# Row sums of absolute values: a partition takes eight neighbouring rows, the transpose goes, and the last row is loaded and reduced in pieces

## Chip, cores, metric

One core of one Trainium2 chip. The metric is the device time of one execution in microseconds (us), the median over repeated executions. Every run reported here is with a granted TensorE clock of 1.00.

In the profile lines DVE is VectorE, ACT is ScalarE, PE is TensorE, and SPq is the queue of SyncE, which issues the DMAs (the transfers between HBM, the chip's main memory, and the on-chip memory of 128 partitions). A packet is the piece of a DMA that one of the core's 16 DMA engines moves at a time. A load has landed when all its packets have; an instruction that waits for it can then start.

## What is computed

```python
batch, dim = 1024, 4096
x = np.random.randn(batch, dim).astype(np.float32)      # fixed seed
out = np.sum(np.abs(x), axis=-1).astype(np.float32)     # shape (1024,)
```

The input has 16.78 MB, the output 4 KB.

## The kernel before

Row 128t+p of the input goes to partition p as its tile t. The last tile (t = 7) is loaded in two parts: its first 3072 columns before everything else, its last 1024 columns after everything else. VectorE sums columns 0 to 3071 of each tile, ScalarE the other 1024. The sums then lie across partitions in an order that the output hasn't; TensorE transposes them into 8 rows of 128. The code here is shortened; "..." marks what is left out.

```python
x_t = x.rearrange("(t p) m -> t p m", p=P)
out_v = out.rearrange("(t p) -> t p", p=P)
v_cols = (dim * 3) // 4
...
nc.sync.dma_start(out=x_tiles[last][:, :v_cols], in_=x_t[last, :, :v_cols])
for t in range(ntiles - 1):
    nc.sync.dma_start(out=x_tiles[t], in_=x_t[t])
nc.sync.dma_start(out=x_tiles[last][:, v_cols:], in_=x_t[last, :, v_cols:])

for t in range(ntiles):
    nc.vector.tensor_reduce(out=sums_v[:, t:t+1], in_=x_tiles[t][:, :v_cols], ...)   # abs, add
for t in range(ntiles):
    nc.scalar.activation(out=chunk, in_=chunk, func=Abs, accum_out=sums_s[:, t:t+1])
nc.vector.tensor_add(out=sums_all, in0=sums_v, in1=sums_s)
nc.tensor.transpose(sums_T_psum, final_sums, identity)
nc.vector.tensor_copy(out=out_sbuf, in_=sums_T_psum)
nc.sync.dma_start(out=out_v, in_=out_sbuf)
```

Of the kernel before, what the change touches and what calls it, by code (L numbers as in the profile page):

```python
# [1 line left out]

# [5 lines left out]


@with_exitstack
def kernel(
    ctx: ExitStack,
    tc: tile.TileContext,
    x: bass.AP,
    axis: int,
    out: bass.AP,
):
    nc = tc.nc
    P = nc.NUM_PARTITIONS  # L20

    batch, dim = x.shape
    assert axis in (-1, 1), f"only the last-axis reduction is supported, got {axis}"
    assert batch % P == 0, f"batch ({batch}) must be a multiple of {P}"

    ntiles = batch // P

    x_t = x.rearrange("(t p) m -> t p m", p=P)
    out_v = out.rearrange("(t p) -> t p", p=P)

    v_cols = (dim * 3) // 4
    if ntiles == 1 or dim < 256:
        v_cols = dim
    s_cols = dim - v_cols

    data_pool = ctx.enter_context(tc.tile_pool(name="data", bufs=1))
    acc_pool = ctx.enter_context(tc.tile_pool(name="acc", bufs=1))
    psum_pool = ctx.enter_context(tc.tile_pool(name="psum", bufs=1, space=bass.MemoryType.PSUM))

    identity = acc_pool.tile([P, P], mybir.dt.float32)  # L40
    make_identity(nc, identity)

    sums_v = acc_pool.tile([P, ntiles], mybir.dt.float32)
    if s_cols > 0:
        sums_s = acc_pool.tile([P, ntiles], mybir.dt.float32)
    sums_all = acc_pool.tile([P, ntiles], mybir.dt.float32)

    x_tiles = [
        data_pool.tile([P, dim], x.dtype, name=f"x_tile_{t}", bufs=1)
        for t in range(ntiles)  # L50
    ]

    last = ntiles - 1
    if s_cols > 0:
        nc.sync.dma_start(out=x_tiles[last][:, :v_cols], in_=x_t[last, :, :v_cols])  # L55
    else:
        nc.sync.dma_start(out=x_tiles[last], in_=x_t[last])

    for t in range(ntiles - 1):
        nc.sync.dma_start(out=x_tiles[t], in_=x_t[t])  # L60

    if s_cols > 0:
        nc.sync.dma_start(
            out=x_tiles[last][:, v_cols:], in_=x_t[last, :, v_cols:]
        )

    for t in range(ntiles):
        nc.vector.tensor_reduce(  # L68
            out=sums_v[:, t : t + 1],
            in_=x_tiles[t][:, :v_cols],  # L70
            axis=mybir.AxisListType.X,
            op=mybir.AluOpType.add,
            apply_absolute_value=True,
        )
    if s_cols > 0:
        for t in range(ntiles):
            chunk = x_tiles[t][:, v_cols:]
            nc.scalar.activation(  # L78
                out=chunk,
                in_=chunk,  # L80
                func=mybir.ActivationFunctionType.Abs,
                accum_out=sums_s[:, t : t + 1],
            )

    if s_cols > 0:
        nc.vector.tensor_add(out=sums_all, in0=sums_v, in1=sums_s)  # L86
        final_sums = sums_all
    else:
        final_sums = sums_v

    sums_T_psum = psum_pool.tile([ntiles, P], mybir.dt.float32)
    nc.tensor.transpose(sums_T_psum, final_sums, identity)  # L92

    out_sbuf = acc_pool.tile([ntiles, P], mybir.dt.float32)
    nc.vector.tensor_copy(out=out_sbuf, in_=sums_T_psum)  # L95

    nc.sync.dma_start(out=out_v, in_=out_sbuf)


# [1 line left out]
_INS = ['x', 'axis']  # L101
_OUTS = [((1024,), 'float32')]
#: Inputs that are plain numbers.
_NUMBERS = {'axis': -1}


# [26 lines left out]
```

## Time and profile before

| What | us | Where it is read |
|---|---|---|
| median time | 50.14 (50.00 to 50.22, 15 runs) | runs |
| span of the profiled run | 48.33 | page |
| first load lands | 7.45 | timeline: VectorE's first reduction starts |
| last load lands | 42.91 | timeline: ScalarE's last ACTIVATE starts |
| store issued | 46.16 | timeline |
| store landed | 47.42 | semaphore records |

### The profile page before, as it was taken

The numbers are of one execution on the slowest core, as the hardware profiler recorded it, in microseconds if no ns is written. First come the engines' busy times: TensorE is split into PE (matmuls) and PEld (weight loads), VectorE is DVE, ScalarE is ACT, GpSimd is POOL, SyncE is SP. The second block draws the span as 40 slices with busy tenths as digits, with TensorE's granted clock in tenths as the row PEclk, the third lists the DMA queues.
The fourth block names the chain that finished last, engine by engine and source line by source line (L and its number), as shares of the span: only waits on it lengthen the run. The fifth ranks groups of instructions, "written<-read, shape, count | busy, mean of one in ns | idle before, by whom it ended". The sixth has DMA issues, their size and how long they took to land.

```text
span 48.3 us, 93 instructions
## 1 busy us (share of the span) xinstructions
PE 0.4 (1%) x1; PEld 0.1 (0%) x1; DVE 27.3 (56%) x10; ACT 10.5 (22%) x17; POOL 0.7 (1%) x6
## 2 busy tenths in 40 slices
PE   0000000000000000000000000000000000000300
PEld 0000000000000000000000000000000000000000
DVE  0000008990899079907990699169915992599410
ACT  3600000000810071007200620063005300594000
POOL 5000000000000000000000000000000000000000
DMA  0779999999999999999999999999999998800000
GB/s 0 132 264 356 407 414 434 434 434 420 434 434 434 434 434 434 407 434 434 434 434 420 434 434 434 420 434 420 434 434 434 434 420 342 346 3 0 0 3 0
DMA packets 1312, 16.78 MB, mean 347 GB/s; under 512 B 152, under 2 KB 160, under 8 KB 288
## 3 DMA queue, kind: packets, MB, share of 16 engines
q1 hardware_dynamic: 1312, 16.78, 83.4%
HBM read 16.78 MB, written 0.00 MB: 347 GB/s over the span
## 4 chain that ended last, share of the span: by engine, by line
DMA 77%; DVE 8%; SPq 7%; issue 1%; PE 1%; DVEq 0%
DMA x_tile<-in_x_dram 77%; DVE sums_v L68 7%; SPq L60 6%; SPq L55 1%; PE sums_T_psum L92 1%; DVE out_sbuf L95 1%; DVE sums_all L86 0%; DVEq L86 0%
## 5 line engine op out<-in xcount | busy, mean ns | idle before, releaser
L68 DVE TENSOR_REDUCE sums_v<-x_tile 128x1 f32<-128x3072 f32 x8 | 26.8, 3353 | 18.2 <-DMA x_tile<-in_x_dram 18.2
L78 ACT ACTIVATE x_tile<-x_tile 128x1024 f32<-128x1024 f32 x8 | 8.5, 1057 | 32.8 <-DMA x_tile<-in_x_dram 32.7
L78 ACT ACTIVATION_READ_ACCUMULATOR x_tile<-x_tile 128x1 f32 x8 | 1.5, 186 | 0.0
L78 ACT ACT_TABLE_LOAD x1 | 1.3, 1283 | 0.7 <-PEq L114 0.7
L92 PE MATMUL sums_T_psum<-identity,sums_all 128*8 128x128 f32 x1 | 0.4, 372 | 45.4 <-DVE sums_all L86 45.4
L95 DVE COPY out_sbuf<-sums_T_psum 8x128 f32<-8x128 f32 x1 | 0.3, 279 | 0.6 <-PE sums_T_psum L92 0.6
masks.py:199 POOL TENSOR_SCALAR_AFFINE_SELECT identity<-identity 128x128 f32<-128x128 f32 x1 | 0.3, 294 | 0.1
L86 DVE TENSOR_TENSOR sums_all<-sums_v,sums_s 128x8 f32<-128x8 f32 x1 | 0.2, 167 | 0.1
masks.py:197 POOL MEMSET identity<- 128x128 f32 x1 | 0.2, 205 | 0.3 <-POOLq L114 0.3
L92 PEld LDWEIGHTS sums_T_psum<-identity,sums_all 128*8 128x8 f32 x1 | 0.1, 83 | 45.4 <-issue 45.4
L114 POOL MEMSET const-float32-0.0<- 128x1 f32 x1 | 0.1, 99 | 0.2 <-issue 0.2
L114 POOL MEMSET const-bfloat16-1.0<- 128x1 bf16 x1 | 0.1, 102 | 0.0
L114 POOL MEMSET const-uint8-127<- 128x1 uint8 x1 | 0.1, 102 | 0.0
L114 POOL MEMSET const-float32-1.0<- 128x1 f32 x1 | 0.1, 99 | 0.0
## 6 DMA issues: line engine op xcount, KB each, us to landing
x_tile<-in_x_dram SPq DMA_DIRECT2D x7, 2048.0 KB, 26.5
x_tile<-in_x_dram SPq DMA_DIRECT2D x1, 1536.0 KB, 6.7
x_tile<-in_x_dram SPq DMA_DIRECT2D x1, 512.0 KB, 35.4
out_dram<-out_sbuf SPq DMA_DIRECT2D x1, 4.0 KB
```

Source lines behind the costliest of these rows:

```text
L55: nc.sync.dma_start(out=x_tiles[last][:, :v_cols], in_=x_t[last, :, :v_cols])
L60: nc.sync.dma_start(out=x_tiles[t], in_=x_t[t])
L68: nc.vector.tensor_reduce(out=sums_v[:, t : t + 1], in_=x_tiles[t][:, :v_cols], axis=mybir.AxisListType.X, op=mybir.AluOpType.add, apply_a ...
L78: nc.scalar.activation(out=chunk, in_=chunk, func=mybir.ActivationFunctionType.Abs, accum_out=sums_s[:, t : t + 1],)
L86: nc.vector.tensor_add(out=sums_all, in0=sums_v, in1=sums_s)
L92: nc.tensor.transpose(sums_T_psum, final_sums, identity)
L95: nc.vector.tensor_copy(out=out_sbuf, in_=sums_T_psum)
L114: nc = _bacc.Bacc("TRN2", target_bir_lowering=False, num_devices=1)
```

## The change

Its intent: without a transpose the result can leave at once, and with the last row cut into small pieces little is left to do when the last byte lands. Partition p holds rows 8p to 8p+7, so its eight sums are neighbours in the output. Rows come in groups of 2, 2, 2 and 1; the eighth row comes in four pieces of falling size, and VectorE and ScalarE share each row about evenly. Core of the diff:

```diff
-    x_t = x.rearrange("(t p) m -> t p m", p=P)
-    out_v = out.rearrange("(t p) -> t p", p=P)
+    x_v = x.rearrange("(p t) m -> p t m", p=P)
+    out_v = out.rearrange("(p t) -> p t", p=P)
...
+    GROUPS = [(0, 2), (2, 4), (4, 6), (6, 7)]
+    CUTS = [(0, 1792), (1792, 2880), (2880, 3712), (3712, 4096)]
+    for a, b in GROUPS:
+        nc.sync.dma_start(out=xt[:, a:b, :], in_=x_v[:, a:b, :])
+    for a, b in CUTS:
+        nc.sync.dma_start(out=xt[:, last, a:b], in_=x_v[:, last, a:b])
...
+    h = (dim * 15) // 32
+    for t in range(last):
+        vec(t, 0, h, sv[:, t : t + 1])
+        act(t, h, dim, ss[:, t : t + 1])
+    vec(last, 0, 896, sv[:, last:])
+    act(last, 896, 1792, ss[:, last:])
+    vec(last, 1792, 2432, v2)
+    act(last, 2432, 2880, s2)
+    act(last, 2880, 3712, s3)
+    nc.vector.tensor_add(out=total[:, :last], in0=sv[:, :last], in1=ss[:, :last])
+    # pre = sv + ss + v2 and pre2 = pre + s2, for the last row
...
+    vec(last, 3712, 4096, v3)
+    # total[:, last] = v3 + s3 + pre2
...
-    nc.tensor.transpose(sums_T_psum, final_sums, identity)
-    nc.vector.tensor_copy(out=out_sbuf, in_=sums_T_psum)
-    nc.sync.dma_start(out=out_v, in_=out_sbuf)
+    nc.sync.dma_start(out=out_v, in_=total)
```

`vec` is the same `tensor_reduce` with absolute values and `act` the same `Abs` ACTIVATE with an accumulator as before.

More of the change, by code (lines that the diff above doesn't have):

```diff
@@ L22 @@
     batch, dim = x.shape
-    assert axis in (-1, 1), f"only the last-axis reduction is supported, got {axis}"
-    assert batch % P == 0, f"batch ({batch}) must be a multiple of {P}"
-    ntiles = batch // P
-    x_t = x.rearrange("(t p) m -> t p m", p=P)
-    out_v = out.rearrange("(t p) -> t p", p=P)
-    v_cols = (dim * 3) // 4
-    if ntiles == 1 or dim < 256:
-        v_cols = dim
-    s_cols = dim - v_cols
-    data_pool = ctx.enter_context(tc.tile_pool(name="data", bufs=1))
-    acc_pool = ctx.enter_context(tc.tile_pool(name="acc", bufs=1))
@@ L38 @@
-    psum_pool = ctx.enter_context(tc.tile_pool(name="psum", bufs=1, space=bass.MemoryType.PSUM))
-    identity = acc_pool.tile([P, P], mybir.dt.float32)
-    make_identity(nc, identity)
-    sums_v = acc_pool.tile([P, ntiles], mybir.dt.float32)
-    if s_cols > 0:
-        sums_s = acc_pool.tile([P, ntiles], mybir.dt.float32)
-    sums_all = acc_pool.tile([P, ntiles], mybir.dt.float32)
-    x_tiles = [
-        data_pool.tile([P, dim], x.dtype, name=f"x_tile_{t}", bufs=1)
-        for t in range(ntiles)
-    ]
@@ L53 @@
-    last = ntiles - 1
-    if s_cols > 0:
-        nc.sync.dma_start(out=x_tiles[last][:, :v_cols], in_=x_t[last, :, :v_cols])
-    else:
-        nc.sync.dma_start(out=x_tiles[last], in_=x_t[last])
-    for t in range(ntiles - 1):
-        nc.sync.dma_start(out=x_tiles[t], in_=x_t[t])
-    if s_cols > 0:
-        nc.sync.dma_start(
-            out=x_tiles[last][:, v_cols:], in_=x_t[last, :, v_cols:]
-        )
-    for t in range(ntiles):
+    nt = batch // P
+    f32 = mybir.dt.float32
+    add = mybir.AluOpType.add
@@ new lines @@
+    x_v = x.rearrange("(p t) m -> p t m", p=P)
+    out_v = out.rearrange("(p t) -> p t", p=P)
+    data = ctx.enter_context(tc.tile_pool(name="data", bufs=1))
+    acc = ctx.enter_context(tc.tile_pool(name="acc", bufs=1))
+    last = nt - 1
+    xt = data.tile([P, nt, dim], f32, name="xt")
+    sv = acc.tile([P, nt], f32, name="sv")
+    ss = acc.tile([P, nt], f32, name="ss")
+    v2 = acc.tile([P, 1], f32, name="v2")
+    v3 = acc.tile([P, 1], f32, name="v3")
+    s2 = acc.tile([P, 1], f32, name="s2")
@@ new lines, with vec @@
+    s3 = acc.tile([P, 1], f32, name="s3")
+    pre = acc.tile([P, 1], f32, name="pre")
+    pre2 = acc.tile([P, 1], f32, name="pre2")
+    total = acc.tile([P, nt], f32, name="total")
+    GROUPS = [(0, 2), (2, 4), (4, 6), (6, 7)]
[4 more added lines that the diff above has]
+        nc.sync.dma_start(out=xt[:, last, a:b], in_=x_v[:, last, a:b])
+    def vec(t, a, b, out_):
@@ L68 @@
         nc.vector.tensor_reduce(
-            out=sums_v[:, t : t + 1],
-            in_=x_tiles[t][:, :v_cols],
+            out=out_,
+            in_=xt[:, t, a:b],
             axis=mybir.AxisListType.X,
-            op=mybir.AluOpType.add,
+            op=add,
             apply_absolute_value=True,
         )
-    if s_cols > 0:
-        for t in range(ntiles):
-            chunk = x_tiles[t][:, v_cols:]
-            nc.scalar.activation(
-                out=chunk,
-                in_=chunk,
-                func=mybir.ActivationFunctionType.Abs,
-                accum_out=sums_s[:, t : t + 1],
-            )
@@ L85, with act @@
-    if s_cols > 0:
-        nc.vector.tensor_add(out=sums_all, in0=sums_v, in1=sums_s)
-        final_sums = sums_all
-    else:
-        final_sums = sums_v
-    sums_T_psum = psum_pool.tile([ntiles, P], mybir.dt.float32)
-    nc.tensor.transpose(sums_T_psum, final_sums, identity)
-    out_sbuf = acc_pool.tile([ntiles, P], mybir.dt.float32)
-    nc.vector.tensor_copy(out=out_sbuf, in_=sums_T_psum)
-    nc.sync.dma_start(out=out_v, in_=out_sbuf)
+    def act(t, a, b, out_):
+        nc.scalar.activation(
+            out=xt[:, t, a:b],
+            in_=xt[:, t, a:b],
+            func=mybir.ActivationFunctionType.Abs,
+            accum_out=out_,
+        )
@@ new lines @@
+    h = (dim * 15) // 32
[8 more added lines that the diff above has]
+    nc.vector.tensor_add(out=total[:, :last], in0=sv[:, :last], in1=ss[:, :last])
+    nc.vector.scalar_tensor_tensor(
+        out=pre, in0=sv[:, last:], scalar=ss[:, last:], in1=v2, op0=add, op1=add
+    )
@@ L101 @@
+    nc.vector.tensor_add(out=pre2, in0=pre, in1=s2)
+    vec(last, 3712, 4096, v3)
+    nc.vector.scalar_tensor_tensor(
+        out=total[:, last:], in0=v3, scalar=s3, in1=pre2, op0=add, op1=add
+    )
+    nc.sync.dma_start(out=out_v, in_=total)
 _INS = ['x', 'axis']
```

## The prediction

> **What bounds the kernel now.** I first read the whole page for its shape, then the chain of work that ended last in order of time, then the timeline of the last 12 us, and at the end the trace's list of DMA packets (each with its size and duration). The page says that this is a stream of 16.78 MB with little work beside it:
>
> ```profile
> DVE  0000008990899079907990699169915992599410
> ACT  3600000000810071007200620063005300594000
> DMA  0779999999999999999999999999999998800000
> GB/s 0 132 264 356 407 414 434 434 434 420 434 434 434 434 434 434 407 434 434 434 434 420 434 434 434 420 434 420 434 434 434 434 420 342 346 3 0 0 3 0
> ```
>
> Each column is 1.2 us. The DMA engines are full from the third slice to the thirty-fifth, at 434 GB/s in the middle; after that there are five slices in which they do nearly nothing. There is a ramp in front, a tail behind, and neither compute engine is busy throughout. The chain in order of time says what the tail consists of (start, duration, what):
>
> ```profile
> 4.19 0.04 issue
> 4.23 37.41 DMA x_tile<-in_x_dram
> 41.64 0.02 issue
> 41.66 3.36 DVE sums_v L68
> ...
> 45.13 0.18 DVE sums_all L86
> 45.31 0.14 issue
> 45.44 0.39 PE sums_T_psum L92
> 45.83 0.02 issue
> 45.85 0.28 DVE out_sbuf L95
> ```
>
> The chain follows the seventh full tile, which lands at 41.66. The reader is to see that everything after 41.66 is serial: a reduction of 3072 columns over all 128 partitions, one addition, a transpose on TensorE, a copy out of PSUM. The timeline adds what the chain does not show, when the very last bytes land and when the result goes out:
>
> ```profile
> 41.66 1.06 ACT L78 ACTIVATE x_tile<-x_tile 128x1024 f32<-128x1024 f32 x1 [3.74 <-DMA x_tile<-in_x_dram]
> 41.66 3.35 DVE L68 TENSOR_REDUCE sums_v<-x_tile 128x1 f32<-128x3072 f32 x1 [1.54 <-DMA x_tile<-in_x_dram]
> 42.63 0.19 ACT L78 ACTIVATION_READ_ACCUMULATOR x_tile<-x_tile 128x1 f32 x1
> 42.91 1.06 ACT L78 ACTIVATE x_tile<-x_tile 128x1024 f32<-128x1024 f32 x1
> ...
> 46.16 0.37 SPq L97 DMA_DIRECT2D out_dram<-out_sbuf  x1
> ```
>
> The 512 KB remainder of the last tile was issued at 7.45 and lands 35.4 us later by the DMA issues, at about 42.9; ScalarE starts on it at 42.91. So the input ends at E = 42.9, the store is issued at 46.16, and E to store is **3.25 us**. From the store's issue to the span's end at 48.3 are 2.15 us, and the measured 50.16 us are 1.85 us above the span; both are in either kernel.
>
> **What the Trainium skill says, and whether the trace agrees.** (1) "VectorE: DVE Perf Modes", the perf-mode tier table: tensor_reduce runs at one element per cycle in every format. The trace agrees: 3353 ns for 3072 columns is 3072/0.96 = 3200 ns plus 153 ns. (2) "ScalarE: Activation LUTs", What ACT_TABLE_LOAD costs: an ACTIVATE with immediates takes 186 ns + 0.833 N. For N = 1024 that is 1039; the trace has 1057, so I use 204 + 0.833 N, plus 0.09 us for the accumulator read of 186 ns, which overlaps by half (42.63 to 42.82 behind an ACTIVATE that ends at 42.72). (3) "DMA: Bandwidth & Descriptors", Latency and other measured facts: copies of 128 rows of 16 KiB keep 207 GB/s each way at a row pitch of 512 KiB but fall to 164 at 2 MiB and 103 at 4 MiB. The change moves the pitch from 16 KB to 128 KB, below all those, so this speaks for no loss; the trace of before, with its 16 KB pitch, cannot confirm it. (4) Same page, Specifications: under 512 B a DMA engine does read-modify-write. The new store has runs of 32 bytes; before had 512, so no line of this trace shows what those cost.
>
> **The change, part by part.** *Layout of the input.* Partition p now holds rows 8p to 8p+7, the bytes are the same, and the stream is the same length if the engines keep their rate. The packets give the rate: 611 ns for 16 KB, 460 ns for the undisturbed ones of 12 KB, 159 ns for 4 KB. That is 0.0368 ns per byte plus about 8 ns a packet, one engine at a time, no gap between DMAs (tiles land every 4.89 us = 8 x 611 ns). Each engine takes 8 of the 128 partitions. The last row of a partition is now cut in four pieces of 7168, 4352, 3328 and 1536 bytes: 272 + 168 + 131 + 65 = 636 ns instead of 611, and eight times that is +0.2 us. Before paid one such cut (460 + 159 - 611 = 8 ns, times 8, is 0.06), so net **+0.15**. Larger packets in front (32 KB if the two rows of a group are one run) give back under 0.1. The start may differ: in before the first DMA's packets of 12 KB took up to 1.56 us and then 460 to 670, so the engines finished them about 1.1 us later than 8 x 460 would have them. About half is latency of the first packet and returns. The rest could come from the odd 12 KB row or from 16 engines starting together; I give it a mean gain of **0.1**.
>
> *The tail.* With E' the landing of the last piece (1536 B x 8 per engine), the earlier landings follow from the packet times: third piece E'-0.52 (8 x 65), second E'-1.57 (8 x 131 earlier), first E'-2.91 (8 x 168 earlier), row 6 E'-5.09 (8 x 272 earlier). VectorE at 153 ns + N/0.96: row 6, 1920 columns, 2.15 us, ends at E'-2.94; 896 columns, 1.09 us, from E'-2.91 to E'-1.82; 640 columns, 0.82 us, from E'-1.57 to E'-0.75. Then three small ops. In before the add of 8 columns took 0.17 and came 0.10 after the reduction, so 0.27 each and 0.8 together: to E'+0.05, hardly later than the last piece. Its 384 columns take 0.55: to E'+0.6. ScalarE: row 6, 2176 columns, 2.02 + 0.09 us, ends at E'-2.98; 896 columns 1.04 us, ends at E'-1.87; 448 columns 0.67 us, ends at E'-0.9; 832 columns 0.99 us from E'-0.52, ends at E'+0.47, ahead of VectorE's 0.6. The last sum of three waits for both: 0.10 + 0.17, so E'+0.87; the store is issued 0.03 later as in before (the copy ends 46.13, issue 46.16): **E'+0.9 to 0.95**. Against E+3.25 this removes **2.3 us**. Of it, cutting the reduction that straddled the end is worth 42.9 to 45.0 less 0.6, about 1.5; add, transpose and PSUM copy (45.03 to 46.13, 1.1 us) against one last sum (0.27) the other 0.8.
>
> *Beside the stream.* Per row VectorE needs 2.15 us and ScalarE 2.11, against 4.89 for the stream, so rows in pairs (4.3 us per 9.8) leave both idle over half the time; the new split of columns is worth nothing until the end. The identity on GpSimd disappears, before 1.3 us and off the path: nothing.
>
> *The store.* 128 runs of 32 bytes over 16 engines in place of 8 runs of 512 over 8. In before those packets took 28 to 53 ns; eight in a row on an engine are about 0.3 us more, with nothing else in flight: **+0.25**.
>
> Sum: 50.16 - 2.3 + 0.15 - 0.1 + 0.25 = 48.16, and I say **48.1 us**.
>
> **The rivals.** *A. The new pitch slows the stream.* The groups stride 128 KB between partitions and the 16 engines work half a megabyte apart. For it: in before the engines spread evenly in time (their first-DMA ends lie 0.57 us apart, one 16 KB packet is 0.61), which looks like streams avoiding one another, and power-of-two pitches are what the skill warns of. Against it: 128 KB is under the pitches where the skill saw a loss, and each run is 32 KB long. Five per cent on 41 us would cost 2 us and eat the gain: 50.2. *B. The wait moves rather than vanishing.* VectorE's order in the tail is up to the scheduler; if a small op that waits for ScalarE's 832 columns stood ahead of the last reduction, the end would be E'+0.47+0.1+0.55+0.54 and 0.8 us would be given back: 48.9. In before the scheduler put the tile that lands first in front, so it orders by readiness, which speaks against this. *C. The end of the stream suffers from small packets and the store from small writes.* Packets of 1536 B and 32 B may have a floor above my line; twice my estimates is +0.4: 48.5. *D. The slow start goes with the 12 KB rows.* Then up to 0.6 us more is won: 47.6.
>
> **Range and chances.** The tail's 2.3 us is built from measured durations and I trust it to 0.3. The start (0.6 either way at most) and the store (0.3) are the next terms; together they make about 0.6 around 48.1. A is the one large risk, at one in ten for more than 1 us, and gives the longer upper arm. So 47.2 to 49.0. Two per cent under 50.16 is 49.16: faster 0.89, same 0.09, slower 0.02.
>
> **What would show it right or wrong.** Right: a middle of the stream at 434 GB/s; input ending within 0.5 us of 42.9; the last VectorE reduction of 384 columns starting within 0.1 us of the last landing; the store issued about 0.9 us after it; about 2.3 us from there to the end. Wrong: GB/s under 420 in the middle slices (A); VectorE's last reduction held by a small op that waits for ScalarE (B); more than 2.6 us from the store's issue to the end, or the four pieces spread over more than 5.5 us (C); an input that ends before 42.3 (D).

## The result

The changed kernel takes **47.13 us** (47.02 to 47.57, 10 runs) against 50.14: a ratio of 0.9412, 95% interval 0.9391 to 0.9434. Ratios are the mean time of one kernel's fast runs over that of the other's fast runs of the same rounds, so not quite the ratio of the medians quoted. The direction was right, and 3.0 us were won where 2.0 were forecast; the time lies just below the range of 47.2 to 49.0.

The first profile of the changed kernel fell on one of its longer runs (47.42). Its busy share of the DMA engines and its GB/s, in 40 slices of 1.14 us:

```profile
DMA  0909999999999979899899999995999899995000
GB/s 0 431 29 460 460 460 460 460 460 460 460 460 431 460 316 402 373 431 431 373 460 460 460 460 460 460 460 230 460 388 431 349 408 397 413 394 207 0 4 0
```

Against before, the ramp at the front looks shorter: the fourth slice is at full rate, where before it took until the seventh. At the end three slices are empty instead of five. Single slices shouldn't be read finely here: packets of 32 KB are booked whole (431, then 29), and the 460 lies above the packets' own rate of 16 x 32768 B / 1213 ns = 432 GB/s. How much of the ramp is really gone is therefore read from the first landing, below. The chain that ended last (start, duration, what):

```profile
4.14 38.38 DMA xt<-in_x_dram
42.51 0.02 issue
42.54 0.56 DVE v L53
...
43.19 0.22 DVE total L84
```

The DMA now runs to 42.5 and 0.9 us of work follow it, where 41.6 and 4.5 us stood before. A second profile of the same kernel, of a run of 47.14 us and so nearer to the median, gives the tail in the timeline:

```profile
37.17 2.15 DVE L53 TENSOR_REDUCE sv<-xt 128x1 f32<-128x1920 f32 x1 [0.68 <-DMA xt<-in_x_dram]
39.51 1.08 DVE L53 TENSOR_REDUCE sv<-xt 128x1 f32<-128x896 f32 x1
40.73 0.82 DVE L53 TENSOR_REDUCE v<-xt 128x1 f32<-128x640 f32 x1
41.65 0.22 DVE L79 SCALAR_TENSOR_TENSOR pre<-sv,ss,v 128x1 f32<-128x1 f32 x1
...
41.79 0.90 ACT L62 ACTIVATE xt<-xt 128x832 f32<-128x832 f32 x1 [0.39 <-DMA xt<-in_x_dram]
42.26 0.55 DVE L53 TENSOR_REDUCE v<-xt 128x1 f32<-128x384 f32 x1
42.59 0.19 ACT L62 ACTIVATION_READ_ACCUMULATOR xt<-xt 128x1 f32 x1
42.92 0.22 DVE L84 SCALAR_TENSOR_TENSOR total<-v,s,pre 128x1 f32<-128x1 f32 x1
43.17 0.35 SPq L87 DMA_DIRECT2D out_dram<-total  x1
```

Row 6 lands at 37.17, and each piece is worked off by about the time the next one lands. The last piece lands at 42.26 and VectorE starts on it at once. ScalarE's piece of 832 columns is read out by 42.78, before VectorE is done at 42.81. The sum of three follows at 42.92 and the store at 43.17, 0.91 us after the last landing. The tail is as predicted (0.90 to 0.95). What differs from the forecast therefore lies ahead of 42.26, in the stream, or behind 43.17, in the store.

### The profile page after: what moved, and what is told of

It is laid out like the page before. It is cut to its first block, busy times and chain, and to the rows that moved or that the text cites. A ratio compares the mean times of both kernels' runs of the same rounds, so it can differ in the third digit from the quotient of the medians.

```text
span 45.6 us, 94 instructions
## 1 busy us (share of the span) xinstructions
DVE 17.9 (39%) x14; ACT 18.4 (40%) x21; POOL 0.2 (0%) x4
## 4 chain that ended last, share of the span: by engine, by line
DMA 84%; SPq 7%; DVE 2%; issue 1%; DVEq 0%
DMA xt<-in_x_dram 84%; SPq L48 4%; SPq L50 3%; DVE v L53 1%; DVE total L84 0%; DVEq L84 0%
## 5 line engine op out<-in xcount | busy, mean ns | idle before, releaser
L62 ACT ACTIVATE xt<-xt 128x2176 f32<-128x2176 f32 (+3 forms) x10 | 16.5, 1648 | 23.9 <-DMA xt<-in_x_dram 23.9
L53 DVE TENSOR_REDUCE sv<-xt 128x1 f32<-128x1920 f32 (+1 forms) x8 | 15.9, 2015 | 24.5 <-DMA xt<-in_x_dram 24.5
L62 ACT ACTIVATION_READ_ACCUMULATOR xt<-xt 128x1 f32 x10 | 1.9, 186 | 0.0
L53 DVE TENSOR_REDUCE v<-xt 128x1 f32<-128x640 f32 (+1 forms) x2 | 1.4, 686 | 0.6 <-DMA xt<-in_x_dram 0.4
```

What stands on the lines that cost most here:

```text
L53: nc.vector.tensor_reduce(out=out_, in_=xt[:, t, a:b], axis=mybir.AxisListType.X, op=add, apply_absolute_value=True,)
L62: nc.scalar.activation(out=xt[:, t, a:b], in_=xt[:, t, a:b], func=mybir.ActivationFunctionType.Abs, accum_out=out_,)
```

## The experiments

A measure for the start of the stream is needed. I take the **start overhead**: the landing of the first DMA less the time of its packets on one engine when they run undisturbed (8 packets, one for each of the engine's 8 partitions, of 460 ns for 12 KB, 611 for 16 KB, 1213 for 32 KB in the list of DMA packets that each trace keeps; 16 packets where two rows of a partition aren't adjacent in memory). Before it is 7.45 - 8 x 0.460 = 3.77 us, in the first profile of the changed kernel 12.80 - 8 x 1.213 = 3.10. That is already 0.67 us of the 1.0 that I missed. Three theories for it:

- **P**: pieces of 12 KB of a 16 KB row run badly wherever they stand, and the change has none of them at the start.
- **Q**: at the start of any stream the 16 engines disturb one another, and small packets take longer to get over it.
- **L**: only the addresses count; rows that are close together in HBM (16 KB from one partition to the next) start slowly, rows 128 KB apart do not.

All runs in one table, times in us. The landings, the store and the span are those of one profiled execution, the median time is that of all. "First packets" are the size of the first DMA's packets, "pitch" the distance in HBM between the rows of neighbouring partitions.

| Run | first packets, pitch | first landing | overhead | last landing | store issued | span | median time |
|---|---|---|---|---|---|---|---|
| before | 12 KB, 16 KB | 7.45 | 3.77 | 42.91 | 46.16 | 48.33 | 50.14 |
| b_12k_second | 16 KB, 16 KB | 8.40 | 3.51 | 42.88 | 46.13 | 48.30 | 50.12 |
| b_loads_only | 12 KB, 128 KB | 6.84 | 3.16 | 42.35 | 45.59 | 47.77 | 49.51 |
| b_layout | 12 KB, 128 KB | 6.71 | 3.03 | 42.23 | 44.64 | 46.90 | 48.69 |
| b_dead_pe | 12 KB, 128 KB | 6.84 | 3.16 | 42.33 | 44.75 | 47.09 | 48.86 |
| changed kernel, first profile | 32 KB, 128 KB | 12.80 | 3.10 | 42.54 | 43.44 | 45.64 | 47.13 |
| a_oldlayout | 16 KB, 16 KB | 13.11 | 3.33 | 42.98 | 43.89 | 46.09 | 47.88 |
| a_pitch32k | 32 KB, 32 KB | 13.05 | 3.35 | 42.42 | 43.33 | 45.53 | 47.30 |
| a_flat32k | 32 KB, 128 KB | 12.89 | 3.19 | 42.29 | 43.19 | 45.40 | 47.15 |
| a_again | 32 KB, 128 KB | 12.85 | 3.15 | 42.26 | 43.17 | 45.36 | 47.12 |
| a_first16k | 16 KB, 128 KB | 7.97 | 3.08 | 42.20 | 44.45 | 46.66 | 48.50 |
| a_first12k | 12 KB, 128 KB | 6.69 | 3.01 | 42.12 | 43.02 | 45.22 | 47.19 |
| a_uncut2 | 32 KB, 128 KB | 12.69 | 2.99 | 41.88 | 44.34 | 46.54 | 48.41 |
| a_fused | 32 KB, 128 KB | 12.81 | 3.11 | 42.20 | 42.90 | 45.10 | 46.87 |

Three of these runs put sums in the wrong place on purpose (a_oldlayout, a_pitch32k, b_loads_only). They still compared as correct: sums of 4096 absolute normals have a mean of 0.798 x 4096 = 3268 and a spread of 0.603 x 64 = 39, so that two rows typically differ by one or two per cent and the comparison didn't see the exchange.

How far single profiles scatter can be read from the table: five profiles with 32 KB first at a pitch of 128 KB have overheads of 2.99 to 3.19, four with 12 KB at that pitch 3.01 to 3.16.

### b_12k_second: the 12 KB rows in second place

```diff
+    nc.sync.dma_start(out=x_tiles[0], in_=x_t[0])
...
     nc.sync.dma_start(out=x_tiles[last][:, :v_cols], in_=x_t[last, :, :v_cols])
...
-    for t in range(ntiles - 1):
+    for t in range(1, ntiles - 1):
```

> The kernel before with its first two loads exchanged: 16 KB rows of tile 0 first, the 12 KB part of the last tile second. Start overhead = landing of the first DMA minus 8 undisturbed packets of it; it was 7.45 - 8 x 0.460 = 3.77 us before and 12.80 - 8 x 1.213 = 3.10 after. Theory P (only 12 KB pieces of 16 KB rows run badly, wherever they stand): overhead of the first DMA 3.1, the second DMA takes 4.2 to 4.5 us instead of 3.7 between the two landings, time 50.1 as before. Theory Q (the start of any stream is disturbed until the 16 engines have spread out in time, and small packets take longer over it): overhead 3.4 to 3.7, the 12 KB packets then run at 460 ns, 3.7 us between the landings, time 49.8 to 50.1.

VectorE's first two reductions in the timeline of this run (start, duration, what; each starts as its load lands):

```profile
8.40 3.35 DVE L69 TENSOR_REDUCE sums_v<-x_tile 128x1 f32<-128x3072 f32 x1 [8.40 <-DMA x_tile<-in_x_dram]
12.22 3.35 DVE L69 TENSOR_REDUCE sums_v<-x_tile 128x1 f32<-128x3072 f32 x1 [0.46 <-DMA x_tile<-in_x_dram]
```

The 12 KB load takes 3.82 us between the landings, near the 3.7 of theory Q and far from the 4.2 of P: in second place such packets run well. The start with 16 KB packets has an overhead of 3.51, as Q has it. But the time is 50.12, unchanged: what the first landing gains on before, the second load loses. P falls; the old layout starts slowly with full rows too. Q stands so far, L too.

### a_first12k: the changed kernel with 12 KB packets first

```diff
-    GROUPS = [(0, 2), (2, 4), (4, 6), (6, 7)]
+    x_f = x_v.rearrange("p t m -> p (t m)")
+    xt_f = xt.rearrange("p t m -> p (t m)")
+    FLAT = [(0, 3072), (3072, 16384), (16384, 24576), (24576, 28672)]
...      # one dma_start for each range of FLAT
```

> The changed kernel with its first DMA cut to 12 KB of row 0 (the second takes the other 52 KB up to row 3, then rows 4 and 5, then 6): packets of 12 KB first, at the new pitch. Theories P and Q: overhead 3.6 to 3.8 as before, time 47.7 to 47.8. Theory L (pitch): overhead 3.1, time 47.1.

VectorE's first reduction in this run:

```profile
6.69 2.15 DVE L55 TENSOR_REDUCE sv<-xt 128x1 f32<-128x1920 f32 x1 [6.69 <-DMA xt<-in_x_dram]
```

And in the kernel before:

```profile
7.45 3.35 DVE L68 TENSOR_REDUCE sums_v<-x_tile 128x1 f32<-128x3072 f32 x1 [7.45 <-DMA x_tile<-in_x_dram]
```

Both wait for a first load of 12 KB per partition, issued at 0.73 and 0.74, and the one with rows 128 KB apart lands 0.76 us earlier. Overhead 3.01, time 47.19. Theories P and Q both said 3.6 to 3.8 and 47.7 or more; only L said this.

### a_first16k: one row in the first group

```diff
-    GROUPS = [(0, 2), (2, 4), (4, 6), (6, 7)]
+    GROUPS = [(0, 1), (1, 3), (3, 5), (5, 7)]
```

> The changed kernel with row groups of 1, 2, 2, 2 rows instead of 2, 2, 2, 1: the first DMA has packets of 16 KB at the new pitch of 128 KB. Theory P (12 KB pieces alone are bad) and theory L (the old pitch of 16 KB is bad): overhead 3.1, time 47.1 to 47.2. Theory Q (size of the first packets): overhead 3.4 to 3.7, time 47.5 to 47.8.

The overhead is 3.08, again with L against Q, and the stream ends at 42.20. But the time is 48.50, 1.3 us above what P and L said and 0.7 above the upper end of Q: a fault of my edit. VectorE in the timeline:

```profile
37.12 5.20 DVE L53 TENSOR_REDUCE sv<-xt 128x1 f32<-128x1920 f32 x3 [5.53 <-DMA xt<-in_x_dram]
42.24 0.81 DVE L53 TENSOR_REDUCE v<-xt 128x1 f32<-128x640 f32 x1
...
43.56 0.55 DVE L53 TENSOR_REDUCE v<-xt 128x1 f32<-128x384 f32 x1
44.21 0.22 DVE L84 SCALAR_TENSOR_TENSOR total<-v,s,pre 128x1 f32<-128x1 f32 x1
```

The last group now brings rows 5 and 6 together at 37.12. VectorE's three reductions from there (rows 5 and 6 and the first piece of row 7) run on to 42.3, past the last landing at 42.20; the later pieces queue behind them, and the last reduction starts at 43.56, 1.36 us after its data. The store comes 2.25 us after the last landing instead of 0.91. The run shows by accident that row 6 must come by itself: that small last group is worth 1.3 us.

### a_oldlayout: the changed kernel with the old row order

```diff
-    x_v = x.rearrange("(p t) m -> p t m", p=P)
+    x_v = x.rearrange("(t p) m -> p t m", p=P)
```

> The changed kernel reading its rows in the old order (row 128t+p to partition p), so the pitch is 16 KB and packets are 16 KB in all row groups; the sums come out in the wrong order on purpose. 24 more packets per engine at 8 to 9 ns are +0.2 us in any theory. Theory L (old pitch bad at the start): overhead 3.7, time 47.9 to 48.0. Theory P: overhead 3.1, time 47.3 to 47.4. Theory Q: overhead 3.4 to 3.7, time 47.6 to 48.0.

47.88 us, 0.75 more than the changed kernel. Of this 0.2 are the 24 additional packets per engine, and the overhead of 3.33 gives another 0.2. The rest is not in the start: in this profile packets of 4352 bytes late in the stream took up to 472 ns instead of 168, and the last landing was at 42.98. Whether such late disturbances belong to the old order stays open; all four executions took 47.69 to 47.93, more than the 47.5 that the two other terms give. The time fits L and Q alike; the overhead is lower than either had said for this pitch.

So the "only" in L isn't shown. At 128 KB the size of the first packets makes no clear difference (2.99 to 3.19), but at the old pitch the overhead is 3.77 with 12 KB, 3.51 with 16 KB and 3.33 here, where the first load is larger and also reads the two rows of a partition from places 2 MB apart. The runs don't separate these two. For this kernel the new pitch is thus worth only about 0.2 us at the start (3.33 against 3.15).

### a_pitch32k and a_flat32k: nothing but the addresses

```diff
-    x_v = x.rearrange("(p t) m -> p t m", p=P)
+    x_v = x.rearrange("(g p r) m -> p g r m", p=P, r=2)   # pitch 32 KB, packets of 32 KB as in the changed kernel
...      # and the indices of the loads to match
```

a_flat32k is the changed kernel with its row groups written as flat column ranges: the same packets, instructions and addresses.

> The changed kernel with the same 32 KB packets, the same order and the same store, but row 256g+2p+r on partition p, so that the pitch between partitions is 32 KB instead of 128 KB (sums come out in the wrong order on purpose). Only the addresses in HBM differ. Theory L (rows packed closely together make the start slow): start overhead 3.3 to 3.7 us against 3.10, time 47.4 to 47.8. Theory Q (only packet sizes matter): overhead 3.1, time 47.1.

> The changed kernel again, with its row groups written as flat column ranges: the same packets and instructions. It is the repeat against which the others of this call are read, and its profile tells whether the late disturbance in the stream of the first profile (packets of 7168 bytes at up to 372 ns) belongs to the kernel: if it was chance, the last landing is at 42.2 instead of 42.53. Time 47.1 either way.

VectorE's first reductions with a pitch of 32 KB:

```profile
13.05 4.21 DVE L53 TENSOR_REDUCE sv<-xt 128x1 f32<-128x1920 f32 x2 [13.05 <-DMA xt<-in_x_dram]
```

With 128 KB (the repeat):

```profile
12.89 4.21 DVE L55 TENSOR_REDUCE sv<-xt 128x1 f32<-128x1920 f32 x2 [12.89 <-DMA xt<-in_x_dram]
```

0.16 us between the landings, and 47.30 against 47.15 us; the ratios to before are 0.9439 (0.9425 to 0.9453) and 0.9412 (0.9398 to 0.9426), intervals that only touch, though the single times do not (47.27 to 47.32 against 47.12 to 47.22). Packets, order and instructions are the same, so this speaks for the addresses alone, if with less than L had said: about a quarter of what 16 KB against 128 KB makes (0.62, next run). It is a weak sign by itself, since the first landings of the five profiles at 128 KB already spread from 12.69 to 12.89. The repeat also answers its own question. Its last landing is at 42.29, and its packets of 7168 bytes took at most 280 ns: the late disturbance of the first profile, which put the landing at 42.54, isn't in every execution. (Nor is it in that one alone: a_again has five packets of 4352 bytes of 245 to 408 ns, which didn't delay its last landing of 42.26.)

### b_loads_only: the kernel before with new addresses and nothing else

```diff
-    x_t = x.rearrange("(t p) m -> t p m", p=P)
+    x_t = x.rearrange("(p t) m -> t p m", p=P)
```

> The kernel before with nothing but the new addresses of its loads (row 8p+t to partition p; pitch 128 KB): same packets, same columns, transpose, copy and store stay (sums come out in the wrong order on purpose). Theory L: first landing at about 6.7 instead of 7.45 (overhead 3.0), time 50.11 - 0.7 = 49.4 to 49.5. If the 0.7 us came with the missing transpose or the missing work on GpSimd: first landing 7.4, time 50.1.

```profile
6.84 3.35 DVE L68 TENSOR_REDUCE sums_v<-x_tile 128x1 f32<-128x3072 f32 x1 [6.84 <-DMA x_tile<-in_x_dram]
...
42.35 1.06 ACT L78 ACTIVATE x_tile<-x_tile 128x1024 f32<-128x1024 f32 x1
```

These lines are VectorE's first reduction and ScalarE's last ACTIVATE, from the timelines of the two engines; their counterparts of before started at 7.45 and 42.91. One line of code, the same packets in the same order, the transpose still there: the first load lands 0.61 us earlier, the last one 0.56, and the median falls by 0.62 (50.13 to 49.51, ratio 0.9873, 0.9859 to 0.9886). **What L says of the addresses is shown, for this kernel: its stream starts later with rows 16 KB apart than with rows 128 KB apart, and that is worth 0.6 us.** In the list of packets the 128 packets of the first DMA ran over their undisturbed time by 0.97 us per engine before and by 0.63 here (sums over all packets, divided by 16). The sixteen packets that started first account for the same in both (0.56 and 0.55 per engine); what vanished is most of the disturbance of those after them. The sixteenth packet also started at 2.27 instead of 2.83, so some engines seem to begin earlier (the list doesn't name a packet's engine), and the mean landing of the 16 engines comes 0.62 us earlier.

### b_layout and b_dead_pe: transpose and store

```diff
+    x_t = x.rearrange("(p t) m -> t p m", p=P)
+    out_v = out.rearrange("(p t) -> p t", p=P)
...
-    make_identity(nc, identity)
...
-    nc.tensor.transpose(sums_T_psum, final_sums, identity)
...
-    nc.vector.tensor_copy(out=out_sbuf, in_=sums_T_psum)
-    nc.sync.dma_start(out=out_v, in_=out_sbuf)
+    nc.sync.dma_start(out=out_v, in_=final_sums)
```

This is b_layout. In b_dead_pe the identity, the transpose and the copy stay and nobody uses them.

> One part alone: the kernel before with the new row order (pitch 128 KB) and without transpose and PSUM copy; its columns, its loads and their order stay (12 KB packets first, the last reduction of 3072 columns stays). Theory L: start overhead 3.0 to 3.1 instead of 3.77, and transpose and copy save 0.75 to 0.8 us from the add to the store: 48.6 to 48.7. Theory P or Q (12 KB packets are to blame): overhead stays 3.77, 49.3 to 49.4. From the store's issue to the end: 2.15 to 2.2.

> The run b_layout with transpose and PSUM copy left in, but the store taking the sums directly in 32-byte runs, so that they are beside the path. Store's issue to landing 1.43 us as in every run with the new store (1.26 with the old). If the end of the program after that landing is shorter in the changed kernels because TensorE has nothing to be waited for, it is 0.91 us here as in before, otherwise 0.77 to 0.84. Time 48.7 to 48.8.

The end of b_layout in the timeline, and its store in the DMA issues (line, engine, KB, us to landing):

```profile
44.44 0.17 DVE L82 TENSOR_TENSOR sums_all<-sums_v,sums_s 128x8 f32<-128x8 f32 x1
44.64 0.35 SPq L87 DMA_DIRECT2D out_dram<-sums_all  x1
```

```profile
out_dram<-sums_all SPq DMA_DIRECT2D x1, 4.0 KB, 1.4
```

b_layout takes 48.69 us, within the expectation: about 0.62 of the 1.42 us gained are the addresses, and the store follows the add by 0.20 us (44.44 to 44.64) where it took 1.03 before (45.13 to 46.16), 0.83 for transpose and copy. In 32-byte runs the store takes 1.43 us from issue to landing against 1.26. The span's end follows that landing by 0.91 us before, 0.83 in b_layout, 0.91 in b_dead_pe (48.86 us, 0.06 above its expectation), and 0.77 in every form of the changed kernel. So with transpose, copy and identity left in as dead work the end is as long as before. Most of the 0.14 us that the changed kernel saves there can be seen in the instruction records: after the wait that the store's landing ends, SyncE still works off two further waits before (at 47.46 and 47.52 us) and in b_dead_pe, one in b_layout (at 46.11) and none in a_again, and each takes about 0.06 us from its start to that of the next.

### a_uncut2: the last row in one piece

```diff
-    CUTS = [(0, 1792), (1792, 2880), (2880, 3712), (3712, 4096)]
+    CUTS = [(0, 4096)]
     ...        # one vec of 1920 columns and one act of 2176 for the last row, then one tensor_add
```

> The changed kernel with the last row loaded in one piece and reduced by one VectorE and one ScalarE instruction (1920 and 2176 columns), one add, then the store. The stream ends 0.2 us earlier (8 x 25 ns), the store comes 2.15 + 0.27 + 0.03 = 2.45 us after the last landing instead of 0.91. Time 47.13 + 1.54 - 0.2 = 48.4 to 48.5. If the cutting is worth less than I think (rival: what is won is the transpose and the balance of columns), 47.6 or less.

```profile
41.88 2.15 DVE L53 TENSOR_REDUCE sv<-xt 128x1 f32<-128x1920 f32 x1 [2.73 <-DMA xt<-in_x_dram]
44.15 0.17 DVE L73 TENSOR_TENSOR total<-sv,ss 128x8 f32<-128x8 f32 x1
```

These are VectorE's last two instructions. The last load lands at 41.88, the store comes at 44.34: 2.46 us, as expected, and 48.41 us in all. From row 6 to the end the stream takes 4.88 us (37.00 to 41.88), with pieces 5.09 (37.17 to 42.26 in a_again): the cutting costs 0.21 us of stream and saves 1.55 behind it.

### a_fused and a_again: a version that beats both

Six columns behind the data hold the partial sums of the last row. They are sums of absolute values, hence positive, so the last reduction, which takes absolute values, can simply include them.

```diff
+    xt = data.tile([P, W + 6], f32, name="xt")           # W = nt * dim, six columns more
...
+    C = [B, B + 1968, B + 3136, B + 3712, W]             # B = last * dim
...
+    for i, v in enumerate((984, 600, 320)):
+        vec(C[i], C[i] + v, xt[:, W + 2 * i : W + 2 * i + 1])
+        act(C[i] + v, C[i + 1], xt[:, W + 2 * i + 1 : W + 2 * i + 2])
...
+    vec(C[3], W + 6, total[:, last:])
```

> An attempt to beat both: the changed kernel with the partial sums of the last row written into six columns behind the data, so that the last reduction (384 columns and those six) writes the result itself and no sum of three follows it; pieces of 1968, 1168, 576 and 384 columns, so that each is done when the next lands. The store comes 0.6 us after the last landing instead of 0.91: 46.8 to 46.9. Rival: the last reduction waits for ScalarE's share of the third piece and half the gain is lost: 47.0.

> The changed kernel itself on the same chip, for the comparison with a_fused: 47.1 to 47.2; last landing between 42.2 and 42.5.

The end of a_fused in the timeline:

```profile
40.98 1.24 DVE L51 TENSOR_REDUCE xt<-xt 128x1 f32<-128x600 f32 x2 [0.26 <-DMA xt<-in_x_dram]
...
41.74 0.42 ACT L60 ACTIVATE xt<-xt 128x256 f32<-128x256 f32 x1
42.06 0.19 ACT L60 ACTIVATION_READ_ACCUMULATOR xt<-xt 128x1 f32 x1
42.31 0.56 DVE L51 TENSOR_REDUCE total<-xt 128x1 f32<-128x390 f32 x1
42.90 0.35 SPq L77 DMA_DIRECT2D out_dram<-total  x1
```

46.87 us (ratio to before 0.9345, 0.9332 to 0.9358) against 47.12 for the changed kernel on the same chip (0.9389, 0.9376 to 0.9402): 0.5% better than the change and clear of it. The store comes 0.70 us after the last landing (42.20 to 42.90), not 0.60. The last reduction started at 42.31, just after ScalarE's accumulator read ended at 42.25 and 0.11 us after its own data. That looks like the rival, right in kind and wrong in size; but VectorE had itself only just finished its reduction of 320 columns (40.98 + 1.24 = 42.22), so no run here separates the two.

## Why the prediction was off

By the steps of its sum, each with what it said and what the runs measured:

| Step | said | measured | from |
|---|---|---|---|
| tail, last landing to store | -2.3 | -2.34 | 3.25 to 0.91 (a_again) |
| cut of the last row | +0.15 net | +0.15 net | 0.21 (a_again against a_uncut2), less the 0.06 of the old cut (from packet times) |
| start of the stream | -0.1 | -0.62 | b_loads_only |
| larger packets | "under 0.1" of gain, not in the sum | -0.22 | 24 packets fewer per engine at 9 ns (2 x 611 against 1213); two rows take 9.78 us between landings in a_oldlayout, 9.71 in a_again |
| store and end | +0.25 | +0.03 | landing +0.17, end after it -0.14 |
| sum | -2.0 | -3.0 | 50.14 to 47.13 |

The -0.62 is what the pitch is worth in the kernel before. With the larger first loads it is worth about 0.2 at the start (a_oldlayout), so pitch and size of the first loads share this row, and the runs give no unique division.

**The tail was right**, and with it the whole mechanism for which the change was made; its two parts as well: cutting the last row saves 1.55 us behind the last landing (said 1.5), transpose and copy 0.83 (said 0.8, with one sum on either side). Rival B didn't come true (VectorE's last reduction waited for no small op), nor did C but for 0.17 us of the store: the pieces of 1536 bytes took 65 ns, exactly on the line of the prediction.

**The step that failed is "I give it a mean gain of 0.1" for the start.** The prediction saw in the trace that the first DMA took about 1.1 us longer than its packets should (0.97 by the count above), put half of it down to latency of the first packet (a part of that size, 0.55 us, indeed stays in b_loads_only; that it is latency isn't shown), and looked for the cause of the rest in "the odd 12 KB row or ... 16 engines starting together". Neither is enough: 12 KB packets start as well as others at the new pitch (a_first12k), and 16 engines start together in every run. It took the old pitch of 16 KB; the prediction considered the pitch only as a danger of the new layout (rival A). Rival D, "the slow start goes with the 12 KB rows", had about the right size (0.6) with the wrong cause; its sign, an input that ends before 42.3, came in a_again (42.26), so that sign didn't tell the causes apart.

**The larger packets** were simply under-counted. With its own 8 ns the prediction would have had 24 x 8 = 0.19 us of gain, where it said "under 0.1" and left it out of the sum.

**The store** was over-priced: the prediction carried over 28 to 53 ns for packets of 512 bytes to packets of 32 bytes, which took 7 to 9 ns (its own line, 0.0368 ns per byte and 8 ns, would have given 9). The landing came 0.17 us later nevertheless, and a shorter end of the program took nearly all of that back.

The three errors had the same sign and added to 0.96 us (0.52, 0.22 and 0.22), while the range took start and store together as about 0.6 and had no term for the packets. One reading of the page was loose besides: in the third slice the DMA engines aren't yet full (0.7 busy, 264 GB/s), and 434 GB/s comes in the seventh.

What stays open: why rows 16 KB apart start slowly. The runs show that the addresses do it, with an effect that is small at 32 KB and depends on the first loads; no run shows whether the engines contend for a part of the memory at all, nor for which. The pitch and the stretch of memory that a load covers (2 MB at 16 KB, 16 MB at 128 KB) always changed together, so which of the two counts isn't shown either.

## What to carry to other kernels

When a stream bounds the kernel, cut its last piece so that each part is worked off as the next one lands, let the last group ahead of it be small, and move sums that don't need the last bytes ahead of them; then one short instruction is left. A layout chosen for the sake of the output is also a layout of the reads: compare the first landing with the undisturbed time of its packets, and try the other layout by itself, in one line, before putting a difference down to anything else. Where an unexplained microsecond stands in the profile of before, forecast both its staying and its going with real weight rather than a mean near zero.

## What the Trainium skill lacked or had wrong

- "DMA: Bandwidth & Descriptors", Latency and other measured facts, gives losses for power-of-two row pitches from 2 MiB up. It has nothing on pitches under 512 KiB: here a pitch of 16 KB cost 0.62 us at the start of the stream against 128 KB (b_loads_only, 49.51 against 50.13 us), with a tile landing every 4.89 us afterwards in both. At 128 KB no loss was seen, which fits its figures.
- The same page, Specifications, says that under 512 B the engines do read-modify-write and miss line rate. It gives no time for a small store issued from SyncE: here 128 packets of 32 bytes took 7 to 9 ns each, and the 4 KB store landed in 1.43 us against 1.26 with 8 packets of 512 bytes. Whether they were read first, no run shows.
- The same page has no measured time of one packet of a DMA issued from SyncE by its size (its fit and its time per packet are for DMAs issued from GpSimd); here 65, 131, 159, 168, 272, 460, 611 and 1213 ns for 1536, 3328, 4096, 4352, 7168, 12288, 16384 and 32768 bytes, which is 0.0368 ns per byte and about 8 ns a packet.
- "VectorE: DVE Perf Modes" (the perf-mode tier table) and "ScalarE: Activation LUTs" (What ACT_TABLE_LOAD costs) held for what was used of them: 3072 columns in 3353 ns and 1920 in 2152, which is 1.04 ns for each further column, the one per cycle at 0.96 GHz of the prediction, and ACTIVATEs of 2176 columns in 2.02 us against 1.999 by the formula.
